# Gated DeltaNet and RWKV-7 on one core: another order of the projections by stretch, and other slots for the first recurrences

## The chip, the core and the metric

The kernel runs on one core of a Trainium2 chip. The core has five engines with an instruction stream each: PE (TensorE, matmuls, with its weight loads shown apart as PEld), DVE (VectorE), ACT (ScalarE), POOL (GpSimd) and SP (SyncE, which issues the DMAs). Each works through its own stream in order and waits for semaphores of the others. The metric is the device time of one execution in microseconds (us), lower is better.

## What is computed

A trunk of two layers over 1104 tokens: 16 meta tokens and 1024 prompt tokens of one sequence, and 8 sampled sequences of 8 tokens. Layer 0 is a gated DeltaNet, layer 1 an RWKV-7. The change is in layer 0 alone:

```python
proj = xn @ w_in                                   # q, k, v, z and two gates
qkv, new_buf = causal_conv(qkv, conv_buf, conv_w)  # four taps, then SiLU
q, k = l2norm(q), l2norm(k)                        # 8 heads, each used by 2 value heads
L = strict_lower(einsum(kb, k) * decay)            # per chunk and value head
u, wk = solve(I + L, [vb, kb * exp(gc)])
def step(S, ...):                                  # over chunks
    v_new = u_c - w_c @ S
    o = qd_c @ S + a_c @ v_new
    S = S * exp(g_last) + kd_c^T @ v_new
y = (rmsnorm(o) * silu(z)) @ w_out
```

All numbers are float32. Every large matmul of the projections is done as three with operands split into a high and a low part.

## The kernel before

**Pairs and products.** Layer 0 works by pairs: pair j (0 to 7) is one key and query head with its two value heads. Each pair needs six products of the normed input with 128 columns of the weight matrix: keys (k), queries (q), the values of its two heads (v, w) and the gates z of its two heads (x and y in the new code). `product` (L435) does one: three segments of up to 384 columns, each in two halves of 12 matmuls. A half is a **slot**. The 48 products are 288 slots, numbered from -24. While a product runs, the weights of the next one are loaded (`raw_weights`, two buffers) and split on ACT and POOL (`next_weights`).

**Order.** The generator `products()` in `layer0` (L2161) fixes PE's order: pair 0 has k q v w in slots -24 to -1; every later pair j has a stretch of 36 slots from `base[j]` = 36 (j - 1), in which it runs k of pair j, the two z of pair j - 1, then q, v, w of pair j. At the end come the two z of pair 7. All other work is hung between the slots by `at(u, f)` (L935): it is emitted behind the last slot that starts before u. PE and ACT run in exactly this order; the streams of DVE, POOL and SP are ordered by the framework's scheduler at build time from what is ready and what was emitted first.

**What follows a product.** k, q, v and w go through `conv` (L493): ACT copies the accumulator, ACT and DVE do four taps (three `cvy` instructions on DVE, L523), DVE the SiLU (L529). z needs only a tanh on ACT and one DVE instruction (L831), which also reads the accumulator; the accumulators of the products have two buffers.

**The front of a pair** (`front_events`, L995). From the keys: decays, scores, then the inverse of 72 blocks of 32 x 32 (`inverse32`, L556): 31 rounds of two dependent DVE instructions (L570, L572), emitted two or three rounds at a time at the times in the list `inv`. `spread` (at `sp`) emits what is left, copies the transposed inverse (L740), writes it to DRAM (`g_t`, `g_u`) and reads it back into `T1n` and the four tiles `TT`. The merges `y32`, `u32`, `y64`, `u64` on PE, at 6.5, 4.5, 3.5 and 1.5 slots before the pair's first recurrence, put the blocks together. The first reads `T1n`.

**The recurrence of a pair** (`chain_events`, L938; `gdn_recur`, L846) starts at slot `first[j]` and takes 27 steps in as many slots, three for each of nine groups of 128 tokens: X and S on DVE, w and o on ACT, the rest on PE; X, w and S have priority. Norms and outputs follow (`gdn_norm_out`); the last are 31.5 slots behind the start. Here `first` = 9, 43, 78, 114, 150, 186, 222, 258. The steps of the inverse are kept behind the last X or S that was emitted before them (`issue_after`).

**Names in the prediction.** b is `base[j]`; in the new code kb, qb, va and vb are the slots in which k, q, v and w start, a is `first[j]`, a0 is `first[j - 1]`. `e`, `k` and `inv` are the slots of the decays, the scores and the steps of the inverse; `ss` and `rd` those at which the states of the samples are loaded and read.

Of the kernel before, what the change touches and what calls it, by code (L numbers as in the profile page):

```python
# [24 lines left out]
QF = 0  # L25

# [9 lines left out]
class Builder:  # L36
# [8 lines left out]
    def t(self, pool, shape, tag, bufs=1, dt=F32):  # L45
        self.uid += 1
        return pool.tile(shape, dt, name=f"{tag}_{self.uid}", tag=tag, bufs=bufs)
# [579 lines left out]
    def gdn_queries(self, j, G, xh, xl, after=None):  # L627
        def dst(s):
            G.Q[s] = self.t(self.kp, [128, 384], "Q", 4)
            return G.Q[s]  # L630
        return self.product(128 * j, "q", xh, xl, self.conv(G.H, 1, j, dst), after)
# [214 lines left out]
    def gdn_recur(self, j, G):  # L846
# [7 lines left out]
        for tg in range(9):  # L854
# [6 lines left out]
            o = t(gp, [128, 2, 128], "o", 6)  # L861
# [3 lines left out]
            X, w = [t(gp, [128, 128], "X", 2) for h in hs], [t(gp, [128, 128], "w", 5) for h in hs]  # L865
# [54 lines left out]
    def gdn_events(self, G, open_, gate, swap):  # L920

        self.events = {}
        base = [36 * (j - 1) for j in range(9)]
        first = [9, 43] + [base[j + 1] + 6 for j in range(2, 8)]
        for u in (-22.9, -19.4, -16.8, -16.7, -16.6):
            self.at(u, gate)
        self.at(-13, swap)
        for j in range(8):
            self.chain_events(j, G, first[j])
            if j:  # L930
                self.front_events(j, G, base[j], base[j] + 18, first[j], open_, base[j] + max(0.3, first[j - 1] - base[j] - 3.4))
            else:
                self.front_events(0, G, -24, -18, first[0], None, None)

    def at(self, u, f, *a):  # L935
        self.events.setdefault(u, []).append(lambda: f(*a))
# [58 lines left out]
    def front_events(self, j, G, b, qb, a, open_, e):  # L995
# [9 lines left out]
        va = qb + 6  # L1005
        at(b + 0.1, lambda: self.gdn_prep(j, g()))
        if j:
            at(b - 5.7, open_, j)
            at(b - 1.4, lambda: self.history_turn(g().H))
            k = max(b + 5.5, e + 4.7)  # L1010
            ed, ee, es = [e + 2 * s for s in range(3)], [k + 2 * s - 1.8 for s in range(3)], [k + 2 * s for s in range(3)]
            inv, per, kk, ss, rd = [k + 9.3 + n for n in range(15)], 2, (b + 11.8, qb + 4.2), b + 13.2, (qb + 6.4, qb + 9.9)
            sp = a - 9.9
# [24 lines left out]
        for h in (0, 1):  # L1038
            for s in range(3):
                at(va + 6 * h + 5.4 + 2 * s, lambda h=h, s=s: self.gdn_value_rows(g(), h, s))  # L1040
        at(va + 12.95, lambda: self.last_tokens(j, g().H))
# [1080 lines left out]
    def layer0(self, top, right, xa, xc):  # L2122
# [38 lines left out]
        def products():  # L2161
            yield from G[0].keys(0)
            yield from self.gdn_queries(0, G[0], kh, kl, 2048)
            yield from self.gdn_values(0, G[0], 0, kh, kl, 2176)
            yield from self.gdn_values(0, G[0], 1, kh, kl, 1152)
            for j in range(1, 8):
                k = 128 * (j + 1)
                z = [4096 + 256 * (j - 1), 4224 + 256 * (j - 1)]
                va = 2048 + 256 * j
                yield from G[j].keys(z[0])  # L2170
                yield from self.gdn_gate(j - 1, G[j - 1], 0, kh, kl, z[1])
                yield from self.gdn_gate(j - 1, G[j - 1], 1, kh, kl, 128 * j)
                yield from self.gdn_queries(j, G[j], kh, kl, va)
                yield from self.gdn_values(j, G[j], 0, kh, kl, va + 128)
                yield from self.gdn_values(j, G[j], 1, kh, kl, 1024 + k if j < 7 else 4096 + 256 * 7)
            yield from self.gdn_gate(7, G[7], 0, kh, kl, 4224 + 256 * 7)
            yield from self.gdn_gate(7, G[7], 1, kh, kl)
# [22 lines left out]
        free = [t(self.kp, [128, 384], n, b) for n, b in (("K", 6), ("K", 6), ("Q", 4))]  # L2200
# [341 lines left out]
```

## Time and profile before

| | |
|---|---|
| runs | 2205.32, 2201.82, 2195.72 us; median 2201.82 us |
| the profiled execution | 2193.46 us, its span on the core 2191.7 us |
| granted clock of TensorE, mean | 0.979 |
| products of layer 0 | from 45 to 1029 us of the span |
| PE busy in them | 929.3 of 983.8 us |

A span is the time from the first to the last instruction of one profiled execution. Busy times are the union of an engine's instructions. PE's matmuls are pipelined, so that the mean time of one (some 340 ns) is longer than the distance to the next. A row of a timeline has start, duration (or the extent of a merged group), engine, line, operation, the tiles written and read, shapes and count; a bracket has the idle time before it and what ended it. A row of the waits has the waiting engine and line, what it waited for, the total, the count and the longest.

### The profile page before, as it was taken

How to read it: one execution, taken by the hardware profiler on the slowest of the kernel's cores; microseconds unless marked ns; L12 is line 12 of the kernel's file. 1: busy time of each engine (PE TensorE's matmuls, PEld its weight loads, DVE VectorE, ACT ScalarE, POOL GpSimd, SP SyncE). 2: the span in 40 equal slices, each digit the busy share in tenths (PEclk: the TensorE clock that was granted, in tenths of full speed). 3: DMA queues.
4: the chain of work that ended last, by engine and by line, in shares of the span. 5: the costliest groups of instructions: out<-in, count | busy, mean ns of one | idle time of the engine just before them, and what ended most of it. 6: DMA issues, size and time to landing. Idle time of an engine off the chain costs nothing. (4 is left out here: it accounts for less than half of the span.)

```text
span 2191.7 us, 54812 instructions
## 1 busy us (share of the span) xinstructions
PE 2051.0 (94%) x20404; PEld 1908.7 (87%) x20404; DVE 1588.0 (72%) x4221; ACT 1291.8 (59%) x3761; POOL 844.7 (39%) x1125
## 2 busy tenths in 40 slices
PE   6869899999999999999899999889999999999997
PEld 5859799899999999999899999889888988888876
DVE  7967869788887979695334676757969657767755
ACT  5526466656566565656633365664847446777774
POOL 3423333334333333334231362344534344444444
PEclk9979999999999999999999999899999999999998
DMA  4423342333333433335345215655555376677764
GB/s 118 119 58 90 86 111 78 102 90 97 104 105 97 112 83 103 110 98 145 121 125 128 67 53 190 211 168 173 171 168 163 115 222 174 180 229 226 234 178 136
DMA packets 430661, 292.64 MB, mean 134 GB/s; under 512 B 147146, under 2 KB 412987, under 8 KB 430395
## 3 DMA queue, kind: packets, MB, share of 16 engines
q1 hardware_dynamic: 430394, 289.14, 45.9%
q8 instruction: 161, 2.64, 0.5%
q14 instruction: 106, 0.86, 0.1%
HBM read 197.68 MB, written 91.37 MB: 132 GB/s over the span
## 5 line engine op out<-in xcount | busy, mean ns | idle before, releaser
L90 POOL TENSOR_TENSOR wlo<-wraw,whi 128x512 fp32r<-128x512 f32 (+1 forms) x246 | 330.6, 1346 | 469.5 <-ACT whi L86 434.9
L76 PE MATMUL d<-xc,whi 128*128 128x384 f32 (+2 forms) x1006 | 279.7, 336 | 4.6 <-ACT whi L86 3.9
L523 DVE SCALAR_TENSOR_TENSOR cvy<-raw,cw,cvy 128x408 f32<-128x408 f32 (+2 forms) x288 | 192.5, 669 | 20.3 <-ACT cvy L62 18.8
L86 ACT CAST whi<-wraw 128x512 fp32r<-128x512 f32 (+1 forms) x246 | 149.7, 611 | 86.4 <-PE d L76 48.8
L76 PEld LDWEIGHTS d<-xc,whi 128*128 128x128 f32 (+1 forms) x1006 | 183.2, 189 | 7.4 <-ACT whi L86 4.6
L76 PE MATMUL d<-xc,wlo 128*128 128x384 f32 (+3 forms) x476 | 157.4, 339 | 2.6 <-POOL wlo L90 2.6
L76 PE MATMUL dz<-xc,whi 128*128 128x384 f32 (+1 forms) x480 | 153.7, 338 | 0.0
L76 PE MATMUL dv<-xc,whi 128*128 128x384 f32 (+1 forms) x480 | 152.2, 337 | 0.0
L76 PE MATMUL d<-xa,whi 128*128 128x384 f32 (+3 forms) x450 | 143.2, 342 | 1.6 <-DVE xb L1160 1.2
L62 ACT ACTIVATE o<-rA,gcol 128x128 f32<-128x128 f32 x128 | 42.1, 366 | 117.6 <-DVE S L902 117.3
L570 DVE TENSOR_TENSOR invtmp<-invA,invT 72x31 f32<-72x31 f32 (+15 forms) x248 | 102.5, 413 | 3.2
L76 PE MATMUL dv<-xa,whi 128*128 128x384 f32 (+1 forms) x288 | 99.0, 344 | 0.0
L572 DVE TENSOR_TENSOR invT<-invT,invtmp 72x31 f32<-72x31 f32 (+15 forms) x248 | 96.1, 388 | 3.3
L76 PE MATMUL dz<-xa,whi 128*128 128x384 f32 (+1 forms) x288 | 98.5, 342 | 0.0
L76 PEld LDWEIGHTS d<-xc,wlo 128*128 128x128 f32 (+1 forms) x476 | 89.2, 189 | 6.3 <-POOL wlo L90 3.5
L76 PEld LDWEIGHTS dz<-xc,whi 128*128 128x128 f32 x480 | 89.3, 188 | 4.6 <-issue 4.6
L76 PEld LDWEIGHTS dv<-xc,whi 128*128 128x128 f32 x480 | 89.1, 188 | 1.4 <-issue 1.4
L76 PEld LDWEIGHTS d<-xa,whi 128*128 128x128 f32 (+1 forms) x450 | 85.2, 192 | 4.8 <-issue 3.3
L76 PE MATMUL d<-xa,wlo 128*128 128x384 f32 (+3 forms) x252 | 85.6, 340 | 1.4 <-POOL wlo L90 1.4
L76 PE MATMUL dq<-xc,whi 128*128 128x384 f32 (+1 forms) x240 | 78.0, 342 | 3.0 <-ACT whi L86 3.0
L76 PE MATMUL dk<-xc,whi 128*128 128x384 f32 (+1 forms) x240 | 78.6, 347 | 0.0
L62 ACT ACTIVATE mixs<-xb,omu 128x64 f32<-128x64 f32 (+3 forms) x128 | 61.6, 521 | 18.3 <-DVE xc L90 8.6
(523 smaller groups left out, 6829.5 us busy)
## 6 DMA issues: line engine op xcount, KB each, us to landing
wraw<-in_gdn_w_in SPq DMA_DIRECT2D x96, 256.0 KB
wraw<-in_rwkv_w_rkvz SPq DMA_DIRECT2D x80, 256.0 KB
Sb<-in_state_gdn SPq DMA_DIRECT2D x64, 256.0 KB
sldcak<-cakd SPq DMA_DIRECT2D x24, 576.0 KB
wraw<-in_rwkv_w_o SPq DMA_DIRECT2D x42, 256.0 KB
E<-drow SPq DMA_DIRECT2D x24, 384.0 KB
attn<-drow SPq DMA_DIRECT2D x24, 384.0 KB
wraw<-in_gdn_w_out SPq DMA_DIRECT2D x36, 256.0 KB
```

The lines of the kernel that those rows point to most:

```text
L62: return self.nc.scalar.activation(out, in_, func, bias=bias, scale=scale, **kw)
L76: self.nc.tensor.matmul(out, lhsT, rhs, start=start, stop=stop)
L86: nc.scalar.copy(hi, x)
L90: e.tensor_tensor(lo, x, hi.bitcast(F32), op=ALU.subtract)
L523: nc.vector.scalar_tensor_tensor(y[0][:, 0:wd], raw[:, k:k + wd], cw[k], y[0][:, 0:wd], op0=ALU.mult, op1=ALU.add)
L570: nc.vector.tensor_tensor(tmp, A[:, j, j + 1:32].unsqueeze(2).broadcast_to([nb, n, m]), Tv[:, j, 0:m].unsqueeze(1).broadcast_to([nb, n, m] ...
L572: nc.vector.tensor_tensor(Tv[:, j + 1:32, 0:m], Tv[:, j + 1:32, 0:m], tmp, op=ALU.subtract)
```

## The change

The order of the products is written in a table, one string for each stretch, and the times of the front's work are worked out from it. Pair 0's two z now run ahead of pair 1's keys; pair 2's stretch keeps its order; in pair 3's the queries stand between the two z; from pair 4 on the queries follow the keys and both z come behind them. The first recurrences of pairs 0 to 3 start 4, 6, 4 and 1 slots later. The steps of the inverse come at 0.85 of a slot instead of 1, from 0.6 slots earlier behind the scores; `spread` no longer hangs on the pair's own recurrence. The states of the samples are loaded and read by the new places, value rows wait for the previous pair's recurrence where that is later, and the buffers of Q, `o` and `w` go from 4, 6 and 5 to 5, 5 and 4, which takes the same space. No operation is added or removed.

```diff
--- before.py
+++ after.py
@@ -23,6 +23,7 @@
 NEG = -1.0e30
 ZF = 1
 QF = 0
+ORDER = ("kqvw", "xykqvw", "kxyqvw", "kxqyvw", "kqxyvw", "kqxyvw", "kqxyvw", "kqxyvwXY")
 
 
 class Ctx:
@@ -626,7 +627,7 @@
 
     def gdn_queries(self, j, G, xh, xl, after=None):
         def dst(s):
-            G.Q[s] = self.t(self.kp, [128, 384], "Q", 4)
+            G.Q[s] = self.t(self.kp, [128, 384], "Q", 5)
             return G.Q[s]
         return self.product(128 * j, "q", xh, xl, self.conv(G.H, 1, j, dst), after)
 
@@ -858,11 +859,11 @@
             if tt == 0:
                 G.seg[s] = [], t(gp, [128, 3, 2], "ssq", 2)
             os, ssq = G.seg[s]
-            o = t(gp, [128, 2, 128], "o", 6)
+            o = t(gp, [128, 2, 128], "o", 5)
             os.append(o)
 
             e = [col[:, tg, 2, hv(h):hv(h) + 1] for h in hs]
-            X, w = [t(gp, [128, 128], "X", 2) for h in hs], [t(gp, [128, 128], "w", 5) for h in hs]
+            X, w = [t(gp, [128, 128], "X", 2) for h in hs], [t(gp, [128, 128], "w", 4) for h in hs]
             r = [self.ps("r", 3, "A") for h in hs]
             part = lambda h, x: r[h][:, 128 * x:128 * x + 128]
             if tg:
@@ -921,16 +922,13 @@
 
         self.events = {}
         base = [36 * (j - 1) for j in range(9)]
-        first = [9, 43] + [base[j + 1] + 6 for j in range(2, 8)]
+        first = [13, 49, 82, 115] + [base[j + 1] + 6 for j in range(4, 8)]
         for u in (-22.9, -19.4, -16.8, -16.7, -16.6):
             self.at(u, gate)
         self.at(-13, swap)
         for j in range(8):
             self.chain_events(j, G, first[j])
-            if j:
-                self.front_events(j, G, base[j], base[j] + 18, first[j], open_, base[j] + max(0.3, first[j - 1] - base[j] - 3.4))
-            else:
-                self.front_events(0, G, -24, -18, first[0], None, None)
+            self.front_events(j, G, base[j] if j else -24, first[j], first[j - 1] if j else None, open_)
 
     def at(self, u, f, *a):
         self.events.setdefault(u, []).append(lambda: f(*a))
@@ -992,7 +990,7 @@
             for h in (0, 1):
                 at((14.5, 23.5, 30.5)[s] + h, lambda s=s, h=h: self.gdn_norm_out(j, G[j], s, h))
 
-    def front_events(self, j, G, b, qb, a, open_, e):
+    def front_events(self, j, G, b, a, a0, open_):
 
         g, at = lambda: G[j], self.at
         Sb = {}
@@ -1002,15 +1000,20 @@
 
         def read(h):
             self.gdn_sample_read(g(), h, [Sb[h, q] for q in (0, 1)])
-        va = qb + 6
+        kb, qb, va, vb = (b + 6 * ORDER[j].index(c) for c in "kqvw")
         at(b + 0.1, lambda: self.gdn_prep(j, g()))
         if j:
             at(b - 5.7, open_, j)
             at(b - 1.4, lambda: self.history_turn(g().H))
-            k = max(b + 5.5, e + 4.7)
+            e = max(kb + 0.3, a0 - 3.4)
+            k = max(kb + 5.5, e + 4.7)
             ed, ee, es = [e + 2 * s for s in range(3)], [k + 2 * s - 1.8 for s in range(3)], [k + 2 * s for s in range(3)]
-            inv, per, kk, ss, rd = [k + 9.3 + n for n in range(15)], 2, (b + 11.8, qb + 4.2), b + 13.2, (qb + 6.4, qb + 9.9)
-            sp = a - 9.9
+            inv, per = [k + 8.7 + 0.85 * n for n in range(15)], 2
+            sp = max(k + 9 + 15 * 0.85, a0 + 17.2)
+            ss = max(kb + 6, a0 + 3.3)
+            kk = max(kb + 5.3, b + 11.8), qb + 4.2
+            u = max(qb + 6.4, a0 + 9.5)
+            rd = u, u + 3.5
         else:
             ed, ee, es = [-18.5, -18.4, -18.3], [-16, -15.2, -14.4], [-15.2, -14.4, -13.6]
             inv, per, kk, ss, rd = [-11.5 + n for n in range(10)], 3, (-12.2, -12.1), -12.8, (-7.6, -4.1)
@@ -1035,10 +1038,11 @@
         at(rd[0], read, 0)
         at(rd[0] + 0.1, states, 1, 1)
         at(rd[1], read, 1)
-        for h in (0, 1):
-            for s in range(3):
-                at(va + 6 * h + 5.4 + 2 * s, lambda h=h, s=s: self.gdn_value_rows(g(), h, s))
-        at(va + 12.95, lambda: self.last_tokens(j, g().H))
+        for s in range(3):
+            for h, v in ((0, va), (1, vb)):
+                u = max(v + 5.4 + 2 * s, a0 + 9 * s + 5.8 + 0.2 * h if j else -99)
+                at(u, lambda h=h, s=s: self.gdn_value_rows(g(), h, s))
+        at(vb + 6.95, lambda: self.last_tokens(j, g().H))
 
     def gdn_norm(self, j, G, s, os, ssq):
 
@@ -2159,22 +2163,22 @@
         self.gdn_events(G, open_, lambda: next(gate, None), swap)
 
         def products():
-            yield from G[0].keys(0)
-            yield from self.gdn_queries(0, G[0], kh, kl, 2048)
-            yield from self.gdn_values(0, G[0], 0, kh, kl, 2176)
-            yield from self.gdn_values(0, G[0], 1, kh, kl, 1152)
-            for j in range(1, 8):
-                k = 128 * (j + 1)
-                z = [4096 + 256 * (j - 1), 4224 + 256 * (j - 1)]
-                va = 2048 + 256 * j
-                yield from G[j].keys(z[0])
-                yield from self.gdn_gate(j - 1, G[j - 1], 0, kh, kl, z[1])
-                yield from self.gdn_gate(j - 1, G[j - 1], 1, kh, kl, 128 * j)
-                yield from self.gdn_queries(j, G[j], kh, kl, va)
-                yield from self.gdn_values(j, G[j], 0, kh, kl, va + 128)
-                yield from self.gdn_values(j, G[j], 1, kh, kl, 1024 + k if j < 7 else 4096 + 256 * 7)
-            yield from self.gdn_gate(7, G[7], 0, kh, kl, 4224 + 256 * 7)
-            yield from self.gdn_gate(7, G[7], 1, kh, kl)
+            todo = []
+            for j in range(8):
+                for c in ORDER[j]:
+                    if c == "k":
+                        todo.append((1024 + 128 * j, lambda w, j=j: G[j].keys(w)))
+                    elif c == "q":
+                        todo.append((128 * j, lambda w, j=j: self.gdn_queries(j, G[j], kh, kl, w)))
+                    elif c in "vw":
+                        h = "vw".index(c)
+                        todo.append((2048 + 128 * (2 * j + h), lambda w, j=j, h=h: self.gdn_values(j, G[j], h, kh, kl, w)))
+                    else:
+                        h = "xyXY".index(c)
+                        i, h = j - 1 + h // 2, h % 2
+                        todo.append((4096 + 128 * (2 * i + h), lambda w, i=i, h=h: self.gdn_gate(i, G[i], h, kh, kl, w)))
+            for n, (_, f) in enumerate(todo):
+                yield from f(todo[n + 1][0] if n + 1 < len(todo) else None)
 
         def before(u):
             while True:
@@ -2197,7 +2201,7 @@
         out, stage = ExitStack(), ExitStack()
         sp = pool("stage", stage, side="right")
         sb = [t(sp, [128, 512], f"stage{k}") for k in range(2)]
-        free = [t(self.kp, [128, 384], n, b) for n, b in (("K", 6), ("K", 6), ("Q", 4))]
+        free = [t(self.kp, [128, 384], n, b) for n, b in (("K", 6), ("K", 6), ("Q", 5))]
         ga, gb = self.load_split(free, self.ogd[0:8], kh, kl), self.residual_in(sb, xb)
         for n in range(24):
             next(ga, None)
```

## Prediction

> **What bounds the kernel now.** The first view is the page's list of engines, the second the busy time of each engine over the whole stretch in which the 48 products run (start and length in us, then PE, PEld, DVE, ACT, POOL with instruction counts, clock, DMA share, GB/s).
>
> ```profile
> span 2191.7 us, 54812 instructions
> PE 2051.0 (94%) x20404; PEld 1908.7 (87%) x20404; DVE 1588.0 (72%) x4221; ACT 1291.8 (59%) x3761; POOL 844.7 (39%) x1125
> 45.00:1028.80 983.80, 929.30 (x8021) 881.88 (x8019) 791.51 (x2192) 581.65 (x1882) 354.14 (x535) 0.98 0.36 97
> ```
>
> The product stretch takes 983.8 us, and PE is busy in 929.3 of them: 54.5 us idle. The change adds and removes no matmul, so it can gain these 54.5 us and the time at a low clock behind them, and no more. Which idle time it is, PE's waits and then its timeline at the first merge of each pair say; the bracket has the idle time and what ended it.
>
> ```profile
> PE rY L76 <- DMA T1n<-g_t: 32.7, 6, 20.1
> 141.83 0.31 PE L76 MATMUL rY<-T1n,E 32*32 32x32 f32 x2 [20.10 <-DMA T1n<-g_t]
> 266.23 0.31 PE L76 MATMUL rY<-T1n,E 32*32 32x32 f32 x2 [8.61 <-DMA T1n<-g_t]
> 388.52 0.28 PE L76 MATMUL rY<-T1n,E 32*32 32x32 f32 x2 [2.51 <-DMA T1n<-g_t]
> 509.33 0.85 PE L76 MATMUL rY<-T1n,E 32*32 32x32 f32 x42
> 628.83 1.33 PE L76 MATMUL rY<-T1n,E 32*32 32x32 f32 x72
> ```
>
> Of the 54.5 us, 20.10 + 8.61 + 2.51 = 31.2 are one wait: at the first merge (`y32`) of pairs 0, 1 and 2, PE stands until the transposed inverse has come back from DRAM. Pairs 3 and 4 don't wait. The inverse is 62 dependent DVE steps; here are its last instruction, the copy of line 740, of pairs 0 to 4, and its first step, of pairs 1 to 4.
>
> ```profile
> 136.55 1.03 DVE L740 COPY invA<-invT 72x1024 f32<-72x1024 f32 x1
> 261.04 1.02 DVE L740 COPY invA<-invT 72x1024 f32<-72x1024 f32 x1
> 383.18 1.11 DVE L740 COPY invA<-invT 72x1024 f32<-72x1024 f32 x1
> 502.79 1.11 DVE L740 COPY invA<-invT 72x1024 f32<-72x1024 f32 x1
> 622.27 1.12 DVE L740 COPY invA<-invT 72x1024 f32<-72x1024 f32 x1
> 202.94 0.18 DVE L570 TENSOR_TENSOR invtmp<-invA,invT 72x31 f32<-72x31 f32 x1
> 329.02 0.18 DVE L570 TENSOR_TENSOR invtmp<-invA,invT 72x31 f32<-72x31 f32 x1
> 451.05 0.18 DVE L570 TENSOR_TENSOR invtmp<-invA,invT 72x31 f32<-72x31 f32 x1
> 571.09 0.18 DVE L570 TENSOR_TENSOR invtmp<-invA,invT 72x31 f32<-72x31 f32 x1
> ```
>
> From the end of the copy to the released matmul it is 141.83 - 137.58 = 4.25, 266.23 - 262.06 = 4.17 and 388.52 - 384.29 = 4.23 us: **4.2 us** of DMA that nothing shortens. Pair 3 has 509.33 - 503.90 = 5.4 us there, so 1.2 us to spare, pair 4 also 1.2 (628.83 - 623.39 = 5.4). So the wait is DVE's lateness. The windows from the first step of the inverse to the end of its copy (pair 0: while it ran) show how full DVE is.
>
> ```profile
> 98.10:137.60 39.50, 22.68 (x164) 21.12 (x162) 37.95 (x98) 12.21 (x34) 9.79 (x13) 0.84 0.21 57
> 202.90:262.10 59.20, 53.39 (x408) 51.21 (x406) 57.40 (x157) 35.65 (x121) 20.32 (x31) 0.99 0.27 77
> 329.00:384.30 55.30, 53.69 (x414) 52.40 (x413) 51.13 (x143) 35.13 (x120) 19.02 (x29) 1.00 0.27 81
> 451.00:503.90 52.90, 51.76 (x396) 50.16 (x395) 48.72 (x139) 32.74 (x112) 15.78 (x27) 1.00 0.27 81
> 571.10:623.40 52.30, 51.16 (x389) 49.25 (x389) 49.67 (x139) 32.80 (x112) 15.86 (x27) 1.00 0.28 82
> ```
>
> DVE works 37.95 of 39.5, 57.4 of 59.2, 51.1 of 55.3 us: it is the bound inside these windows, though it has slack over the whole stretch (791.5 of 983.8). The inverse shares it with whatever the products bring at the same time.
>
> **The change, pair 0.** The merge moves from slot 2.5 (first recurrence 9, less 6.5) to 6.5: four slots more for PE. A slot is 12 matmuls; slot 0 ran from the first line to the second:
>
> ```profile
> 113.42 0.42 PE L76 MATMUL dk<-xa,whi 128*128 128x384 f32 x1
> 115.59 0.27 PE L73 MATMUL flast<-ident,last 128*108 128x128 f32 x1
> ```
>
> that is 2.17 us. PE came to the merge at 141.83 - 20.10 = 121.7; four slots at 2.17 (8.7) less about 0.5 for the narrower third segment, plus one set of value transposes that now comes first (0.5), put it at about 130.4. DVE hardly changes: up to slot 0 its work is the same; behind it the three taps of pair 1's first key segment fall out and three z multiplications come in, by these rows of lines over later windows (count, busy us, mean ns, idle):
>
> ```profile
> L831 DVE SCALAR_TENSOR_TENSOR zg<-zg,dz 128x384 f32<-128x384 f32 (+1 forms) x6 | 3.2, 533 | 5.8 <-ACT zg L62 5.8
> L523 DVE SCALAR_TENSOR_TENSOR cvy<-raw,cw,cvy 128x408 f32<-128x408 f32 (+2 forms) x27 | 18.0, 666 | 1.1 <-ACT cvy L62 1.1
> ```
>
> 3 x 0.53 - 3 x 0.67 = -0.4. So the data land at 141.4 instead of 141.8, and the wait is about **11.0 us, not 20.1** (between 9 and 13: a slot's extras are not exactly known). The light z slots relieve DVE only behind the merge, where it had been idle anyway.
>
> **Pairs 1 to 3.** What counts is the distance from the first inverse steps to the merge, in slots, by the formulas: before 19.6 to 36.5 (16.9), 53.6 to 71.5 (17.9), 88.6 to 107.5 (18.9), pair 4 124.6 to 143.5 (18.9). After: pair 1's keys come 12 slots later and its recurrence only 6, so 26.2 to 42.5 (16.3); pair 2, 59 to 75.5 (16.5); pair 3, 92 to 108.5 (16.5); pair 4, 125 to 143.5 (18.5); pairs 5 to 7, 16 to 35.5 of each stretch (19.5, before 18.9). In time, before, from the first step to where PE came to the merge (start:end, length, PE busy, clock, DMA):
>
> ```profile
> 202.90:257.60 54.70, 53.37 (x408) 1.00 0.26 76
> 329.00:386.00 57.00, 54.79 (x419) 1.00 0.28 84
> 451.00:509.30 58.30, 57.16 (x432) 1.00 0.30 85
> 571.10:628.80 57.70, 56.44 (x424) 1.00 0.30 85
> ```
>
> 3.24, 3.18, 3.08 and 3.05 us a slot. New: pair 1 16.3 x 3.24 = 52.8, less about 2 because three steps fewer of pair 0's recurrence lie in it: 51; pair 2 16.5 x 3.18 = 52.5, I take 53 for its later recurrence; pair 3 16.5 x 3.08 = 51; pair 4 18.5 x 3.05 = 56.4; pairs 5 to 7 59.5. **PE has less time before it needs the inverse in pairs 1 to 3, not more.**
>
> What DVE must do in it, as a difference to the windows above (summed durations count 0.85, since they overlap: in pair 1's window the groups of lines sum to 68.2 us in 57.4 busy). Prices, from the groups of pair 1's window:
>
> ```profile
> L902 DVE SCALAR_TENSOR_TENSOR S<-S,eglb,rA 128x128 f32<-128x128 f32 x11 | 3.5, 338 | 0.0
> L822 DVE TENSOR_TENSOR bv<-f,sk 128x384 f32<-128x384 f32 x4 | 2.2, 548 | 0.0
> ```
>
> Pair 1: three taps fewer (-2.0), twelve X, S and o of the recurrence fewer (12 x 0.32 = -3.9), two `bv` more (+1.1), silus -0.5: -5.3, times 0.85 = -4.5; 59.2 - 4.5 = 54.7, and with 4.2 of DMA 58.9 against PE's 51: 7.9. Pair 2: three or four taps more (+2.2), silus +1.0, four recurrence operations fewer (-1.2), two `bv` more (+1.1): +2.6 at 0.85; the quicker pace of the steps (0.85 slot, before 1) closes part of DVE's idle time (4.2 of 55.3; 1.8 is left as in pair 1): 55.3 + 2.6 - 2.4 + 4.2 = 59.7 against 53: 6.7. Pair 3: z adds 1.1, `bv` 1.1, taps and recurrence -1.8: +0.4; 52.9 + 0.4 - 2.4 + 4.2 = 55.1 against 51: 4.1. From each I take 1.6, half of the six taps (6 x 0.64 x 0.85 = 3.3) that come in the last slots and may stand behind the inverse: **6.3, 5.1 and 2.5 us**. Pair 4: 52.3 + 4.2 = 56.5 against 56.4, and at the quicker pace nothing; pairs 5 to 7 have 3 us to spare. Bounds of the three: nothing (DVE puts the inverse first and keeps pairs 3 and 4's spare time), and 12.4, 10.4 and 8.5 (pairs 1 and 2 need pair 1's 59.2, pair 3 needs 55.3, the longest seen).
>
> **The clock** behind a wait (start:end, length, PE busy, granted clock, DMA):
>
> ```profile
> 141.80:149.00 7.20, 6.65 (x86) 0.51 0.30 45
> 266.20:273.00 6.80, 6.33 (x89) 0.59 0.32 49
> 388.50:395.00 6.50, 5.93 (x84) 0.53 0.32 49
> 628.80:636.00 7.20, 6.61 (x102) 1.00 0.38 75
> ```
>
> After each of the three waits PE runs at about half speed; the twelve matmuls of a slot then take some 3.7 us (2.17 by the 0.59), so about 1.5 us go. Four waits cost 6.0, three cost 4.5: +1.5. The Trainium skill, "TensorE: Matmul & The Clock Gate" (Why this matters for your kernels), says that gaps up to some 3 us keep the clock; here the 2.51 us gap lost it too. By the page a wait left at 2.5 us would be free, and the sum 1.5 us lower.
>
> **What else is edited, at nothing.** Q five buffers, `o` five, `w` four: the fifth Q is written 2 slots or more after the recurrence has read its old contents; with four `w`, GpSimd's masked copies of the first token group have 3 slots (some 9 us) instead of 6; without that time ACT would wait and the recurrence with it. The state loads of the samples are issued 4 slots earlier in later pairs, 2 slots before their third buffer comes free: SP would stand some 6 us, with the next weights behind it, which are due a product (18 us) later; uncovered, that would be 6 us a pair. The z of pair 1 overwrites pair 0's last 3.5 slots after its use, where it had 7.5; about 10 us still hide a late write-back. The end is unmoved: the last recurrence starts at slot 258 as before.
>
> **Sum.** Before 31.2; after 11.0 + 6.3 + 5.1 + 2.5 = 24.9; clock +1.5: **-4.8 us**. The profiled execution took 2193.5 us (span 2191.7), the median of the three runs is 2201.8; the difference is put on the median: **2197 us**. A measurement of this kernel can tell about 0.5%, 11 us, from no change.
>
> **Rivals.** *The inverses come in time* (faster, 0.33). DVE's list puts the earlier-issued inverse steps ahead of the taps, and 16.5 slots suffice; only pair 0's wait stays. 31.2 - 11.0 = 20.2, and two clock losses, 3.0, go: 2179. For it: pairs 3 and 4 have 1.2 us to spare, and the spread is issued as many slots ahead of the merge as there. Against it: DVE is already 92 to 97% busy in every window. *Keys, queries and values in one run fill DVE* (slower, 0.17): in the new pair 1 four products with convolutions follow each other, then pair 2's keys. If the inverses need the longest times seen, the waits are 11.0 + 12.4 + 10.4 + 8.5 and pair 4's 55.3 + 4.2 - 56.4 = 3.1, together 45.4, with two clock losses more (3.0): +17, 2219. It decides from about 5 us more per pair than I put. *The wait of pair 0 doesn't shrink* (0.05), since z waits for DVE to free its two accumulators and PE gains no slots: +9 on the forecast, 2206.
>
> **How the numbers follow.** The forecast has 0.45 (its own range 2188 to 2208), the rivals 0.33, 0.17 and 0.05. The range, 2175 to 2213, takes in the faster case and the near half of the slower one. Faster by over 0.5%: 0.33 and a little of the forecast, 0.35; slower: 0.17 and a little, 0.19; within: 0.46.
>
> **What would show it.** Right: `rY` still waits for T1n, about 11 us in pair 0, and pair 3 waits for the first time; pairs 5 to 7 copy earlier before their merge. Wrong: no wait in pairs 1 to 3 (faster), or windows from first step to copy over 59 us (slower). Had PE new waits for accumulators, for weights or for the samples' states, my costs at nothing would be wrong.

## The result, and the profile after

| | before | after |
|---|---|---|
| median of the runs | 2197.12 us (7 runs, 2191.01 to 2205.32) | 2214.91 us (7 runs, 2209.93 to 2221.76) |
| ratio | | 1.0078, 95% interval 1.0057 to 1.0099 |
| profiled execution | 2193.46 us, span 2191.7 us | 2210.89 us, span 2209.2 us |

The change makes the kernel **0.8% slower**, 17.8 us by the medians and 17.4 us by the two profiled executions. The forecast was 2197 us with a range up to 2213: the time lies just above the range, and on the other side of no change than the forecast's -4.8 us. The page's first lines after, and the window of the products (start, end and length in us, then PE, PEld, DVE, ACT and POOL busy with their counts, granted clock, DMA share, GB/s):

```profile
span 2209.2 us, 54805 instructions
PE 2054.3 (93%) x20404; PEld 1915.8 (87%) x20404; DVE 1578.2 (71%) x4221; ACT 1290.6 (58%) x3761; POOL 827.1 (37%) x1125
```

```profile
45.00:1049.80 1004.80, 932.79 (x8022) 888.93 (x8020) 781.99 (x2190) 582.00 (x1881) 337.02 (x535) 0.97 0.35 95
```

The products took 983.8 us and now take 1004.8, 21.0 more. PE is busy 932.8 us (929.3 before: 3.5 of the 21.0) and idle 72.0 (54.5 before: **17.5**). Behind the products lie 1159.4 us, before 1162.9; there the change edits nothing but the buffers of Q that are used again. So nearly all of the loss is PE's idle time among the products. PE's waits name it (waiting line, what it waited for, total us, times, longest):

```profile
PE rY L77 <- DMA T1n<-g_t: 38.6, 8, 13.3
PE rA L77 <- DVE o L914: 8.9, 11, 1.1
PE fsc L77 <- DVE E L710: 5.7, 4, 1.5
PE mhist L74 <- DVE zg L1069: 3.1, 1, 3.1
```

The wait for the inverse, 32.7 us before, is 38.6: not shorter, but **longer by 5.9**. The other 11.6 of the 17.5 us are many small waits, the three largest below it here: the recurrence for `o`, 8.9 (before 5.5), the scores for `E`, 5.7 (before 2.2), and one of 3.1 us for an accumulator that didn't exist before. PE's timeline at the first merges of pairs 0 to 4:

```profile
143.26 0.31 PE L77 MATMUL rY<-T1n,E 32*32 32x32 f32 x2 [12.62 <-DMA T1n<-g_t]
277.25 0.31 PE L77 MATMUL rY<-T1n,E 32*32 32x32 f32 x2 [13.28 <-DMA T1n<-g_t]
401.55 0.28 PE L77 MATMUL rY<-T1n,E 32*32 32x32 f32 x2 [8.38 <-DMA T1n<-g_t]
525.59 0.22 PE L77 MATMUL rY<-T1n,E 32*32 32x32 f32 x2 [2.57 <-DMA T1n<-g_t]
646.57 0.41 PE L77 MATMUL rY<-T1n,E 32*32 32x32 f32 x14
```

Pair 0 waits 12.6 us, not 20.1: PE used the time. But its merge doesn't come earlier (143.3, before 141.8), so what was gained there is no time, only work done in advance. Pairs 1, 2 and 3 then wait 13.3, 8.4 and 2.6 us, before 8.6, 2.5 and none. From merge to merge it is 134.0, 124.3, 124.0 and 121.0 us up to pair 4, before 124.4, 122.3, 120.8 and 119.5. Pair 4's merge stands in the same slot in both kernels and comes 17.7 us later (646.57, before 628.83): **nearly the whole loss is made by then**. Where DVE stood meanwhile, the windows from the first step of each inverse to the end of its copy tell, pairs 0 to 4:

```profile
98.80:139.10 40.30, 30.89 (x215) 29.22 (x212) 38.80 (x99) 13.10 (x35) 9.19 (x12) 0.93 0.23 61
214.90:273.00 58.10, 47.35 (x344) 45.91 (x342) 56.08 (x154) 31.26 (x104) 19.71 (x31) 0.95 0.25 70
338.80:397.10 58.30, 52.15 (x403) 50.16 (x402) 56.16 (x156) 36.49 (x128) 15.56 (x27) 0.99 0.28 78
464.50:519.10 54.60, 48.54 (x339) 47.48 (x339) 48.38 (x133) 30.56 (x106) 14.28 (x21) 0.94 0.22 63
591.50:638.00 46.50, 44.80 (x331) 43.76 (x330) 41.02 (x121) 28.46 (x102) 10.73 (x17) 1.00 0.22 64
```

Pairs 1 and 2 are full: DVE works 56.1 of 58.1 and 56.2 of 58.3 us. In pair 4, where the queries stand early, the inverse takes 46.5 us (before 52.3): there the new order does help, but PE doesn't wait there anyway. The first steps stand 71.7 us behind the previous merge in pair 1 (214.9 - 143.3) and 61.5 in pair 2 (338.8 - 277.3), before 61.1 and 62.8: pair 1's front starts **10 us late**, for its keys now stand behind pair 0's z.

### The profile page after: what moved, and what is told of

Read it like the earlier page. It is cut to its first block, busy times and chain, and to the rows that moved or that the text cites. A ratio compares the mean times of both kernels' runs of the same rounds, so it can differ in the third digit from the quotient of the medians.

```text
span 2209.2 us, 54805 instructions
## 1 busy us (share of the span) xinstructions
PE 2054.3 (93%) x20404; PEld 1915.8 (87%) x20404; DVE 1578.2 (71%) x4221; ACT 1290.6 (58%) x3761; POOL 827.1 (37%) x1125
## 5 line engine op out<-in xcount | busy, mean ns | idle before, releaser
L63 ACT ACTIVATE o<-rA,gcol 128x128 f32<-128x128 f32 x128 | 43.2, 368 | 120.6 <-DVE S L903 120.4
```

What stands on the lines that cost most here:

```text
L63: return self.nc.scalar.activation(out, in_, func, bias=bias, scale=scale, **kw)
```

## The experiments

Three things were changed together: the order (z first in pair 1's stretch, queries early from the fourth on), the first recurrences (13, 49, 82, 115 for 9, 43, 78, 114), and the rest (pace of the inverse's steps, places of the sample loads and value rows, buffers). The explanations that stood against each other: z first starts pair 1's front late; queries early fill DVE or make new waits; the later first recurrences leave too little distance from merge to merge; DVE's share of the convolutions sets the length of the inverse. All were timed in three rounds beside the kernel before; ratios are to it, with 95% intervals. Small diffs are against the kernel after where nothing else is said.

**Keys first again in pair 1.**

```diff
-ORDER = ("kqvw", "xykqvw", "kxyqvw", ...
+ORDER = ("kqvw", "kxyqvw", "kxyqvw", ...
```

> The changed kernel with one string put back: pair 1's stretch is k x y q v w again (keys first), all else as changed. Theory A (the pace is a cycle from merge to merge: a pair's inverse can only start some 61 us after the merge before, if its keys are there; z first makes the keys late, 71.7 us): the first inverse step of pair 1 comes 61 to 63 us after pair 0's merge, its merge 10 us earlier than 277.3, the wait there falls from 13.3 to 0 to 5 us, and the time by 8 to 13 us against the changed kernel, to 1.001 to 1.004 of before. Theory B (four products with convolutions in one run fill DVE): the inverse of pair 1 keeps its 58 us and the wait stays over 10 us; the time falls by less than 4 us. Theory C (the loss is in the small new waits from pair 3 on): no change in the time.

2204.31 us, ratio 1.0059 (1.0036 to 1.0083). Its first merges of pairs 0 and 1:

```profile
147.90 0.31 PE L77 MATMUL rY<-T1n,E 32*32 32x32 f32 x2 [16.75 <-DMA T1n<-g_t]
272.07 0.22 PE L77 MATMUL rY<-T1n,E 32*32 32x32 f32 x2 [2.61 <-DMA T1n<-g_t]
```

z first does two things against each other. Without it pair 1's first step comes 61.6 us behind the merge, not 71.7, and its wait falls to 2.6 us, as theory A had it. But pair 0's merge comes at 147.9, not at 143.3, and the time stays above theory A's 1.001 to 1.004. The window of pair 0's inverse shows why the merge is late:

```profile
98.80:143.70 44.90, 31.09 (x216) 29.40 (x214) 43.24 (x111) 16.15 (x41) 15.61 (x20) 0.89 0.21 57
```

DVE has 12 instructions and 4.4 us more in it than in the kernel after (111 and 43.2, there 99 and 38.8): with the merge four slots later, PE runs on into the keys, and their convolution comes before the inverse is done. By the medians z first costs some 0.2% (1.0078 against 1.0059), inside the intervals. It is not the main cause.

**Queries late again in all stretches.**

```diff
-ORDER = (..., "kxqyvw", "kqxyvw", "kqxyvw", "kqxyvw", "kqxyvwXY")
+ORDER = (..., "kxyqvw", "kxyqvw", "kxyqvw", "kxyqvw", "kxyqvwXY")
```

> The changed kernel with the strings of pairs 3 to 7 put back (k x y q v w, z ahead of the queries); pair 1 keeps z first. Theory A: the waits of pairs 0 to 2 stay at 12.6, 13.3 and 8.4 us; pair 3's grows from 2.6 to some 6 us, since its inverse then shares DVE with three products of convolutions (53 to 55 us instead of less); the time is 0 to 5 us above the changed kernel. Theory C (queries ahead of z make new waits of PE for DVE, at the scores, the z multiplication and the recurrence, some 12 us): those waits go and the time falls by 8 to 12 us.

2216.10 us, 1.0113 (1.0089 to 1.0137). Pairs 5 to 7 now take 123.1, 121.5 and 122.1 us from merge to merge (after 119.8, 118.9, 119.4), with an inverse of 53 us for 46.7. Theory C, by which queries early make waits that go here and some 10 us with them, is refuted: the time does not fall. By the medians queries early are a gain of 0.35%, which the intervals do not separate from nothing, and it is made behind pair 4, whose merge comes 2.5 us earlier here (644.1 for 646.6). z first alone, which is what this kernel has, costs as much against the old order in the next run.

**The old order in all**, with all else of the change.

```diff
-ORDER = ("kqvw", "xykqvw", "kxyqvw", "kxqyvw", "kqxyvw", "kqxyvw", "kqxyvw", "kqxyvwXY")
+ORDER = ("kqvw", "kxyqvw", "kxyqvw", "kxyqvw", "kxyqvw", "kxyqvw", "kxyqvw", "kxyqvwXY")
```

> All strings put back to the old order; of the change stay the later first recurrences, the pace of the inverse, the places of the sample states and the buffers. Theory A: pair 0's merge at 142 to 144 us, pair 1's inverse starts 61 to 63 us behind it, so the cycles are 120 to 124 us as before and the time is within 4 us of before (0.998 to 1.003). Theory B: the same. Theory D (the later first recurrences alone cost, since each window between a pair's scores and its merge is shorter by 1 to 2 slots): waits in pairs 1 to 3 of 5 us each, 1.004 to 1.007 of before.

2209.99 us, 1.0078 (1.0051 to 1.0104): as slow as the kernel after. The order, which names the change, is worth nothing in sum that the intervals show; the loss comes with the two other parts. Theories A and B had this time within 4 us of before and are refuted as causes of the loss; theory D, the later first recurrences, comes nearest. Its waits are not 5 us each, but 2.5, 8.1 and 1.5 in pairs 1 to 3.

**Fewer taps in pair 1's values.**

```diff
-            for k in range(1, 4):
+            for k in range(1, 2 if ft in (18, 19) else 4):
```

> The changed kernel; pair 1's two value products leave out two of their three taps on DVE (the second to fourth weights of the convolution but one), 12 instructions of some 0.65 us, all inside the inverse of pair 1. It measures what the competition on DVE costs. Theory B: the inverse takes 58.1 - 6.5 = 51 to 52 us, pair 1's wait falls from 13.3 to 6 to 7 us, and the time by 5 to 7 us. Theory A (a cycle carries any delay on): the same fall at pair 1, and all later merges, pair 2's among them, come earlier by the same amount. If DVE's list lets the inverse through anyway, nothing changes.

This kernel leaves out two of the three taps that DVE does for each segment of pair 1's values. 2205.92 us, 1.0059 (1.0044 to 1.0074). The first merges of pairs 0 and 1:

```profile
143.07 0.31 PE L77 MATMUL rY<-T1n,E 32*32 32x32 f32 x2 [12.61 <-DMA T1n<-g_t]
269.30 0.31 PE L77 MATMUL rY<-T1n,E 32*32 32x32 f32 x2 [7.30 <-DMA T1n<-g_t]
```

Twelve taps fewer (12 x 0.68 = 8.2 us of DVE) shorten pair 1's inverse by 8.1 us (50.0 for 58.1), its wait by 6.0, and bring its merge 8.0 us earlier (269.3 for 277.3). The cycles behind it stay as they were, so that the merges of pairs 2 and 3 come 7.4 and 8.2 us earlier too (394.1 and 517.4). The price of a tap inside an inverse is its whole duration, not 0.85 of it and not half.

**The rest alone**: old order and old first recurrences.

```diff
+ORDER = ("kqvw", "kxyqvw", "kxyqvw", "kxyqvw", "kxyqvw", "kxyqvw", "kxyqvw", "kxyqvwXY")
-        first = [13, 49, 82, 115] + ...
+        first = [9, 43, 78, 114] + ...
```

> The changed kernel with the old order and the old first recurrences (9, 43, 78, 114): of the change stay the quicker pace of the inverse steps, the places of the sample states and the buffers. If the quicker pace is what makes PE wait for o and X in every pair (122 us a pair instead of 119 in the run with the old order), the pairs from 4 on take 121 to 122 us here too and the time is 1.004 to 1.007 of before. If it is the later firsts that cost, the time is that of before within 0.3%, and pair 0 waits 20 us, pair 1 5 to 9 us.

2203.09 us, 1.0045 (1.0025 to 1.0065). The inverses get shorter (pair 1's 54.3 us, before 59.1; pair 2's 50.9, before 55.3), pair 1 waits 5.9 us and no merge of pairs 2 to 7 more than 0.2. But PE waits for `o` 24 times, before 10 times, by this row of its waits and that of the kernel before.

```profile
PE rA L77 <- DVE o L914: 11.7, 24, 0.8
```

```profile
PE rA L76 <- DVE o L913: 5.5, 10, 0.9
```

Pair 4's merge is 6.1 us earlier than before (622.7 for 628.8); from there a cycle takes 120.9 to 122.8 us, before 118.8 to 119.2, and pair 7's merge is 1.8 us later. In this profiled execution (2198.68 us) the products take 986.3 us, 2.5 more than before: most of the 0.45% isn't located by the trace.

**The first recurrences alone**: the kernel before with the new ones, the buffers, and only those places of samples and value rows that they need.

```diff
-        first = [9, 43] + [base[j + 1] + 6 for j in range(2, 8)]
+        first = [13, 49, 82, 115] + [base[j + 1] + 6 for j in range(4, 8)]
```

> The kernel before with the later first recurrences (13, 49, 82, 115) and what they cannot do without: the buffers, the later loads of the samples' states and later value rows. Pace and order are the old ones. If the later firsts cost through shorter windows, pair 0's merge comes at 146 to 148 us (PE goes on to pair 1's keys, whose taps delay the inverse), pair 1 waits 3 to 9 us, pair 2 6 to 10 us, pair 3 0 to 3 us, and the time is 1.004 to 1.008 of before. If the pace is the cause, the time is that of before within 0.3%.

2222.50 us, **1.0132** (1.0116 to 1.0148): the worst of all.

```profile
147.51 0.31 PE L76 MATMUL rY<-T1n,E 32*32 32x32 f32 x2 [16.71 <-DMA T1n<-g_t]
276.46 0.28 PE L76 MATMUL rY<-T1n,E 32*32 32x32 f32 x2 [7.43 <-DMA T1n<-g_t]
404.80 0.28 PE L76 MATMUL rY<-T1n,E 32*32 32x32 f32 x2 [11.84 <-DMA T1n<-g_t]
530.34 0.26 PE L76 MATMUL rY<-T1n,E 32*32 32x32 f32 x2 [4.37 <-DMA T1n<-g_t]
656.91 0.28 PE L76 MATMUL rY<-T1n,E 32*32 32x32 f32 x2 [2.00 <-DMA T1n<-g_t]
```

All five merges wait; pair 4's comes at 656.9, 28 us later than before. To tell which of the four does it, the same kernel was run with pair 0's alone, and with the other three alone.

```diff
+        first = [13, 43, 78, 114] + [base[j + 1] + 6 for j in range(4, 8)]
```

> The kernel before with only pair 0's first recurrence later (13 instead of 9; buffers, sample loads and value rows as in the run with the later firsts alone). If what costs is that PE runs four slots on and its key taps delay pair 0's inverse, pair 0's merge comes at 146 to 148 us instead of 141.8, pair 1's inverse has 4 slots less of its 17 and waits 10 to 15 us at its merge, pairs 2 and 3 are as before, and the merges from pair 2 on come 5 to 15 us later: 1.003 to 1.008 of before. If PE's four slots were a real gain, the wait of pair 0 falls by 3 to 9 us and the end comes earlier.

2202.12 us, 1.0039 (1.0021 to 1.0056).

```diff
+        first = [9, 49, 82, 115] + [base[j + 1] + 6 for j in range(4, 8)]
```

> The kernel before with only pairs 1 to 3's first recurrences later (49, 82, 115; the rest as in the run with the later firsts alone). Pair 0's merge at 141 to 143 us with a wait of 20 us. Pair 1 has 6 slots more, its wait goes (0 to 1 us). If the distance from one first recurrence to the next (40, 33, 33, 35 slots instead of 34, 35, 36, 36) is what costs, pairs 2 and 3 wait 8 to 12 and 3 to 5 us and pair 4 2 us, and the time is 1.004 to 1.010 of before; if only pair 0's place costs, the time is that of before or 0.3% under it, since pair 1's wait of 8.6 us has gone.

2212.87 us, 1.0089 (1.0059 to 1.0119). The rows of the one with pair 0's alone, then of the other:

```profile
146.50 0.31 PE L76 MATMUL rY<-T1n,E 32*32 32x32 f32 x2 [16.74 <-DMA T1n<-g_t]
265.10 0.28 PE L76 MATMUL rY<-T1n,E 32*32 32x32 f32 x2 [12.08 <-DMA T1n<-g_t]
398.07 0.28 PE L76 MATMUL rY<-T1n,E 32*32 32x32 f32 x2 [2.52 <-DMA T1n<-g_t]
```

```profile
143.07 0.31 PE L76 MATMUL rY<-T1n,E 32*32 32x32 f32 x2 [20.01 <-DMA T1n<-g_t]
273.68 0.50 PE L76 MATMUL rY<-T1n,E 32*32 32x32 f32 x20
397.18 0.28 PE L76 MATMUL rY<-T1n,E 32*32 32x32 f32 x2 [11.86 <-DMA T1n<-g_t]
526.96 0.22 PE L76 MATMUL rY<-T1n,E 32*32 32x32 f32 x2 [4.11 <-DMA T1n<-g_t]
651.11 0.28 PE L76 MATMUL rY<-T1n,E 32*32 32x32 f32 x2 [2.38 <-DMA T1n<-g_t]
```

Pair 0's alone: the merge moves from 141.8 to 146.5 (key taps in the inverse, as without z first). Pair 1's merge, after a wait of 12.1 us, is then 1.1 us earlier than before (265.1 for 266.2); the loss is made behind it, where pair 2's first step comes 72.4 us behind the merge, before 62.8. PE idles 5.9 us in that stretch for 1.1, and its granted clock is 0.91 for 0.96; what makes PE stand there was not tried. The other three alone: pair 1 waits no more, but only because its merge is put later, at 273.7 (before 266.2); pair 2 stands 33 slots behind it, and its wait of 11.9 us takes the saved one's place. 0.4% and 0.9% add up to the 1.3% of all four. A pair's front needs the distance to the merge before, and 33, 33 and 35 slots (49 to 82, 82 to 115, 115 to 150) give less of it than the 35, 36 and 36 before. The parts do not simply add up: with the old first recurrences the rest costs 0.45%, with the new ones it takes the loss from 1.3% to 0.8%.

**Queries early with the old first recurrences**, and the rest as in the kernel after. This follows from the runs so far: keep what helped, undo what cost.

```diff
-ORDER = ("kqvw", "xykqvw", "kxyqvw", "kxqyvw", "kqxyvw", ...
+ORDER = ("kqvw", "kxqyvw", "kqxyvw", "kqxyvw", "kqxyvw", ...
-        first = [13, 49, 82, 115] + ...
+        first = [9, 43, 78, 114] + ...
```

> The part of the change that shortens the inverse, without the parts that lengthen the way to it: first recurrences as before (9, 43, 78, 114), keys first in every stretch, in pair 1 the queries between the two z, from pair 2 on queries ahead of both z; the rest as changed. From the changed kernel's pairs 4 to 7 the inverse takes 46.5 us when z lies in its window. By the cycle (merge to merge 61 us to the inverse, then the inverse, 4.2 us of DMA) pair 2 and later need 112 us and don't wait, pair 1 waits 2 to 6 us, pair 0 20 us as before. Time 0.993 to 0.998 of before.

2185.86 us (5 runs, 2181.09 to 2188.07), **0.9963** (0.9947 to 0.9978): faster than both kernels.

```profile
143.10 0.31 PE L77 MATMUL rY<-T1n,E 32*32 32x32 f32 x2 [20.05 <-DMA T1n<-g_t]
262.86 0.24 PE L77 MATMUL rY<-T1n,E 32*32 32x32 f32 x2 [2.69 <-DMA T1n<-g_t]
```

```profile
326.70:373.70 47.00, 44.71 (x330) 43.67 (x330) 41.13 (x121) 28.41 (x102) 10.51 (x17) 1.00 0.22 65
446.60:489.60 43.00, 42.45 (x318) 41.80 (x317) 39.03 (x116) 27.31 (x98) 11.63 (x16) 1.00 0.22 65
```

Pair 0 waits its full 20 us again, pair 1 2.7, and no merge behind them waits; a cycle takes 119 to 120 us (the last 122). The inverses of pairs 2 and 3 take 47.0 and 43.0 us (before 55.3 and 52.9): z, which brings DVE one instruction a segment in place of taps and SiLU, stands beside them. The whole stretch of the products:

```profile
45.00:1026.50 981.50, 925.47 (x8026) 882.94 (x8023) 791.59 (x2191) 583.39 (x1882) 339.80 (x537) 0.98 0.35 97
```

By these profiled executions only 2.3 of the 7.1 us by which the span is shorter (2184.6 for 2191.7) stand here, and they come from PE's busy time (925.5 for 929.3): PE idles 56.0 us (before 54.5), since the wait for `T1n` falls by 9.1 while those for `E` and `o` rise by 5.3 and 4.0 and 4.8 us of waits for `attn` are new. Pair 4's merge is 7.4 us earlier than before, pair 7's 2.3, as the last cycles are longer. The rest lies behind the products, in a stretch that takes 1157 to 1170 us in the profiled executions of these kernels; that it is a gain of the order is not shown.

**The same with the old pace of the inverse.**

```diff
-            inv, per = [k + 8.7 + 0.85 * n for n in range(15)], 2
-            sp = max(k + 9 + 15 * 0.85, a0 + 17.2)
+            inv, per = [k + 9.3 + n for n in range(15)], 2
+            sp = a - 9.9
```

> The order with queries early and the old first recurrences (the run at 0.9963) with the old pace of the inverse and the old place of its end (one slot a step pair, 9.9 slots ahead of the recurrence). If the quicker pace is what lets the inverse of pairs 2 to 7 end in 43 to 47 us, it takes 50 to 53 us here, still without a wait at the merge; PE's waits at the recurrence fall as in the kernel before. Time 0.993 to 0.998 of before, with pair 1's wait at 4 to 8 us instead of 2.7.

2216.49 us, 1.0101 (1.0084 to 1.0117); a miss, since 0.993 to 0.998 was expected, with fewer waits at the recurrence (for `o` 10.8 us, there 9.5). Cycles take 121.5 to 127.9 us, the inverses of pairs 1 to 7 50.5 to 58.8. The quicker pace is worth 1.4% with queries early (1.0101 against 0.9963), while the rest, to which it belongs, costs 0.45% with the old order. From pair 3 on the inverses take 50.5 to 51.5 us, for 43 to 49: steps that are emitted late leave the room that z makes unused. PE idles 19.0 us more among the products, 9.9 of them at `T1n` and 5.8 in transposes of the values that wait for DVE. Why the later steps bring the latter is not shown.

**z of pair 0 inside pair 0**, to give PE work in its wait of 20 us without keys.

```diff
+ORDER = ("kqXvw", ".kyqvw", "kxqyvw", "kqxyvw", "kqxyvw", "kqxyvw", "kqxyvw", "kqxyvwXY")
+        first = [11, 45, 79, 114] + ...
```

> One z of pair 0 moved into pair 0's own stretch, ahead of the values (k q x v w), pair 1 then k y q v w from slot 6, pair 2 k x q y v w, pairs 3 to 7 k q x y v w; first recurrences 11, 45, 79, 114. Half of pair 0's values' convolutions fall behind its inverse, so pair 0's merge comes at 137 to 140 us instead of 141.8 and its wait falls to 9 to 12 us; pair 1's keys come 6 slots later and its cycle takes 122 to 127 us. Time 0.990 to 0.998 of before; if late keys cost as in the changed kernel (10 us in that cycle for 12 slots), 0.997 to 1.001.

2193.56 us, 0.9994 (0.9981 to 1.0006): no gain; the time is in the range given for late keys. Pair 0's merge was hoped for at 137 to 140 and comes at 141.9, with 15.1 us of wait; pairs 1 and 2 wait 4.8 and 3.2.

All that differ by whole parts, side by side:

| order | first recurrences | pace and rest | ratio |
|---|---|---|---|
| old | old | new | 1.0045 |
| old | new | old | 1.0132 |
| old | new | new | 1.0078 |
| z first alone | new | new | 1.0113 |
| queries early alone | new | new | 1.0059 |
| both (the kernel after) | new | new | 1.0078 |
| queries early, from pair 1 on | old | new | 0.9963 |
| queries early, from pair 1 on | old | old pace | 1.0101 |

## Why the prediction was wrong, step by step

**Right: where to look.** PE's idle time among the products decides, and the wait for `T1n` is its largest part. PE comes to pair 0's merge at 143.26 - 12.62 = 130.6, forecast 130.4; the wait is 12.6, forecast 11.0, as the data land 1.9 us later than put. Pair 3 waits for the first time, and pairs 5 to 7 copy earlier, as the prediction said would show.

The sum put -4.8 us; the products took 21.0 more. Of the 25.8 between, 12.2 are waits for `T1n` (put at -6.3, measured +5.9), 11.6 are waits put at nothing, and 2.0 are PE's busy time (put at +1.5 for the clock, measured +3.5).

**The step that failed: the waits of pairs 1 and 2**, put at 6.3 and 5.1 us and measured at 13.3 and 8.4. Their mechanism was right (less time for PE, DVE full); the term that was mis-sized is DVE's time in their windows. PE's side was near, by the windows from the first step to PE's arrival at the merge of pairs 1, 2 and 3:

```profile
214.90:264.00 49.10, 47.35 (x344) 1.00 0.27 76
338.80:393.20 54.40, 52.15 (x403) 1.00 0.26 75
464.50:523.00 58.50, 52.44 (x364) 0.94 0.25 72
```

49.1 and 54.4, forecast 51 and 53. DVE's side was put too short: 58.1 and 58.3 us from first step to copy, forecast 54.7 - 1.6 = 53.1 and 55.5 - 1.6 = 53.9. Of the two terms that were 5.0 and 4.4 us too short, this was missing:

- In both, the 1.6 us for taps that "may stand behind the inverse", half of six. The windows hold 25 taps each, and the forecast had counted 24 (pair 1) and 25 or 26 (pair 2) before that deduction: none stood behind. The fewer-taps run shows that each counts in full.
- In pair 1, DVE's work fell by 1.3 us (57.40 to 56.08) and not by 4.5. DVE's groups of lines in its window have 31 X, S and o of the recurrence, before 37: six fewer, not twelve. Two taps fell out, not three, and the SiLUs took as long as before (4.5 us).
- In pair 2, DVE's work grew by 5.0 us (51.13 to 56.16) and not by 2.6: three taps, two SiLUs, three `bv` and two operations of the recurrence more, where the forecast had two `bv` more and four such operations fewer. Its taps, before and after:

```profile
L523 DVE SCALAR_TENSOR_TENSOR cvy<-raw,cw,cvy 128x408 f32<-128x408 f32 (+2 forms) x22 | 13.3, 604 | 0.0
L524 DVE SCALAR_TENSOR_TENSOR cvy<-raw,cw,cvy 128x336 f32<-128x336 f32 (+2 forms) x25 | 16.0, 639 | 0.0
```

The kernel before with the new first recurrences alone has 27 taps in pair 2's window, with no fewer SiLUs and `bv`: it is the later recurrence, not the order, that lets more of the values' work fall into the inverse. The 2.4 us put for the quicker pace came nearly in full. DVE's idle time in pair 2's window fell by 2.0 (4.2 to 2.1); with the old order and the new first recurrences it is 3.6 us at the old pace and 2.4 at the quicker.

With the sizes measured, DVE and 4.2 us of DMA against PE give 58.1 + 4.2 - 49.1 = 13.2 and 58.3 + 4.2 - 54.4 = 8.1: **the sum's form holds, its terms were mis-sized**. This is little more than what a wait is, and tests only the 4.2. Pair 1's wait is even above the bound given (12.4), pair 2's below its own (10.4); the forecast took values well below both.

**Pair 3: the number is right by luck, the reason not.** Its wait is 2.57 us, forecast 2.5. But PE came only after 58.5 us, not 51, since it had stood 6.1 us before; DVE's copy was done at 519.11, and 4.2 us of DMA would have given 523.3, a wait of 0.3. The DMA took 6.5. SyncE's timeline there, and in pair 1:

```profile
518.03 0.30 SPq L744 DMA_DIRECT2D g_t<-invT  x1
519.14 0.31 SPq L743 DMA_DIRECT2D g_u<-invA  x1
520.63 0.34 SPq L647 DMA_DIRECT2D attn<-drow  x1
521.12 0.41 SPq L918 DMA_DIRECT2D out_p_gdn<-S  x1
521.62 1.63 SPq L747 DMA_DIRECT2D T1n<-g_t  x3
```

```profile
271.98 0.30 SPq L744 DMA_DIRECT2D g_t<-invT  x1
273.05 0.32 SPq L743 DMA_DIRECT2D g_u<-invA  x1
274.85 1.40 SPq L747 DMA_DIRECT2D T1n<-g_t  x3
```

Two other transfers were issued ahead of the read of `T1n`, which started 3.6 instead of 2.9 us behind `g_t` and released PE 4.0 instead of 2.4 us later (525.59 and 277.25). The other traces fit: in the first-merge waits the way took 6.0 to 7.5 us in the six cases with `attn` or weights issued between write and read, and 3.7 to 5.2 in all others, one of them with a small transfer between. That the transfers are the cause was not tried.

**What was put at nothing** brought about 11.6 us. The longest single one was not among the edits named at all: with the new first recurrence 82, a norm output of pair 2 comes at slot 82 + 24.5 = 106.5 and pair 4's turn of the history at 106.6, and both use the one accumulator `m`. First the kernel after, then the run with pair 0's first recurrence alone, where pair 2's is 78. All seven kernels with 82 have the wait, 2.8 to 3.4 us, and none of the six without it has.

```profile
516.10 0.42 PE L74 MATMUL mhist<-ident,hist 96*128 96x96 f32 x1 [3.14 <-DVE zg L1069]
```

```profile
516.56 0.25 PE L73 MATMUL mhist<-ident,hist 96*128 96x96 f32 x1
```

The buffers, the sample loads and the weights, which the prediction did weigh, cost nothing that the waits show. Of the rest, the waits for `E` come with the early queries (4.5 to 9.5 us in the six kernels that have them, at most 2.2 in the others). Those for `o` are 5.5 to 7.7 us with the old order and the old pace and 6.9 to 12.0 with one of the two or both changed. The fastest version has both, 7.5 and 9.5 us.

**The clock** was put at +1.5 us for one wait more. PE's busy time rose by 3.5. Behind each of the four merges the granted clock is about half, as behind three before (here the first and the last; pairs 1 and 2 have 0.52 and 0.60), and behind the wait for the accumulator it falls too, to 0.77 in the next 6.9 us:

```profile
143.20:150.40 7.20, 6.63 (x85) 6.43 (x86) 2.14 (x6) 0.02 (x1) 0.00 (x0) 0.50 0.32 50
525.60:532.10 6.50, 6.18 (x85) 6.00 (x86) 2.84 (x10) 0.00 (x0) 1.37 (x2) 0.54 0.27 43
```

```profile
516.10:523.00 6.90, 6.90 (x36) 0.77 0.65 183
```

The prediction took the trace's side here against the Trainium skill, "TensorE: Matmul & The Clock Gate" (Why this matters for your kernels), by which gaps up to some 3 us keep the clock. The fourth merge, behind a gap of 2.57 us, is a second case on the trace's side. What was missing is the loss behind a wait that the prediction didn't have.

**The rivals.** The slower one, which had 0.17, comes nearest in its time (2219) and in what it says of DVE: full, with inverses of 58 us in pairs 1 and 2. Its reason is not borne out. It had four products with convolutions in a row fill DVE, and with the old order put back the inverses of pairs 1 and 2 still take 58 us and the time is the same. In pair 4, where it had DVE as late as in the others, the early queries gave room. What neither the forecast nor a rival said is why the wait that pair 0 saves is no gain: its merge is set by DVE (141.0 to 143.1 us in the runs with the old first recurrence and the old order in pair 0, 143.1 to 143.5 with z behind it, 146.5 to 147.9 with keys behind it), and each later pair starts from the merge before. Filling PE's wait in advance did not pay here: the work that follows either came into the inverse (keys) or left pair 1's keys late (z), and the later merges were put at later slots. That it would pay with the later merges moved forward was not tried.

## What to carry to other kernels

Where one engine's wait marks the end of a chain that starts anew from each such end, measure the cycle from end to end on the engine that sets it; work moved into the wait of another engine gained nothing here, as that cycle did not get shorter. Moving one stage's start later to spare its wait shortens the next stage's cycle by the same slots, and the wait turns up there (with 33 slots where 35 had been, pair 2 waited 11.9 us and pair 1 no longer its 8.6). Order work within a cycle so that the stretch in which the bound engine runs its chain holds what costs it least, here z, and emit the chain early enough to use it: either alone lost time, both together gained 0.4%, of which the trace shows about a third in the stretch that was changed.

## What the runs showed of the hardware

The way of the transposed inverse through DRAM, from the end of the copy to the released matmul, took 4.2 us in pair 1 and 6.5 us in pair 3 of the kernel after, where two more transfers were issued between its write and its read. Behind an idle gap of 2.57 us, with the full clock granted ahead of it, TensorE's granted clock was 0.54 over the next 6.5 us. A tap of 0.68 us on DVE inside a dependent chain lengthened the chain by 0.68 us (8.1 us for twelve), though DVE had 2 us of idle time in that window.
